# Seven-product stages: the first two sums of weight blocks put together by an accumulating transfer

## The chip, the cores and the metric

The kernel runs on one core of one Trainium2 chip. The metric is the device time of one execution in microseconds (us), the median of several runs. Five engines work side by side, each on its own list of instructions in a fixed order: TensorE (PE; its weight loads are PEld), VectorE (DVE), ScalarE (ACT), GpSimd (POOL) and SyncE (SP). SP and ACT issue transfers; POOL can issue them too.

## The reference

Two layers of an encoder trunk on 512 tokens of width 1024, float32 throughout. Each layer is a half-step feed-forward block, a mixer of three kinds of attention with gates, and a second half-step feed-forward block:

```python
def swiglu(x, w_gu, w_down):
    gate, up = jnp.split(x @ w_gu, 2, axis=-1)
    return (jax.nn.silu(gate) * up) @ w_down

y = swiglu(rmsnorm(h, ffn1_pre_g[l]), ffn1_w_gu[l], ffn1_w_down[l])
h = h + 0.5 * rmsnorm(y, ffn1_post_g[l])
```

`w_gu` is 1024 x 5632 (2816 gate and 2816 up columns), `w_down` 2816 x 1024. Four such blocks are computed, two per layer. The change lies in `x @ w_gu` of these four.

## The kernel before, in words

Activations lie transposed, features on the 128 partitions and tokens along the row. TensorE's float32 products are made from splits: a value is written as a rounded part `hi` (ScalarE copies it into float32r) and the rest `lo` (VectorE subtracts), and a product takes three matmuls: hi·hi, hi·lo, lo·hi. So each block of weights costs a copy on ScalarE and a subtraction on VectorE before TensorE can use it.

Weights come from device memory as tiles of eight 128 x 128 blocks (512 KB) in the order in which they are used: `wts[i]` is the i-th tile. `fetch` loads one into a buffer of the tag `wr`, of which there are three. The tag `wp` has four buffers of 512 KB; the plain products keep split weights in them.

A feed-forward block has 22 pairs of gate and up columns. The first six (`PLAIN`) are plain products. The other 16 are groups of a scheme with seven products in place of eight: rows are halved into two lots of four blocks, tokens into two halves, and gate and up columns are combined. These 16 groups I call a seven-product stage; there are four of them, one in each feed-forward block. The activations' sums and differences are made once, ahead of the stage. For the weights each group g needs:

- two tiles, fetched by SP in `fetches(g)`. The first, `raws[g][0]`, holds the blocks called 22 and 11; the second, `raws[g][1]`, holds 12 in its first half and the base block-column in its second half.
- `sum13` (L543): `r13` = first tile + base, where the base is used for both halves of the first tile. One VectorE instruction of 128 x 1024 elements. `r13` lies in a buffer of `wp`.
- `high13`, `low13` (L555, L559): the split of `r13`.
- `sum2` (L562): the second half of the second tile becomes `r13`'s second half plus the first tile's first half. `sum4` (L572): the first half of the second tile becomes the sum of its two halves.
- `high1`, `low1` (L547, L551), `high12`, `low12` (L566, L569), `high24`, `low24` (L576, L580): the splits of the first tile, of 12 and of the two later sums. `w12` lies in `wp`, the others in the tag `x` (12 buffers).

A group has the products p1 to p7, each of 12 matmuls (L650). In the loop they come in the order p1(g), p7(g), p3(g-1), p6(g), p4(g), p2(g), p5(g). p1 and p4 use the first tile's split, p7 and p5 that of `r13`, p2 that of 12, p6 and p3 that of the two later sums. Partial results stay in PSUM: `seed` (L689), `copy7` (L693) and `copy2` (L696) copy them out between products on ScalarE, `add21` (L700) and `add22` (L704) add them on VectorE, `silu0`, `silu1` (L708, L711) and `gated` (L716) finish a pair of columns. Because p3(g-1) writes the PSUM bank that `add22(g-1)` reads, it waits for it.

The order in the code is not the order on the engines. A planner works through the whole program when it is built and puts each engine's instructions in order by when it reckons their inputs and buffers to be ready, the earlier in the program first. Then each engine works its list through in that order; an instruction that waits holds up all behind it. So the trace shows instructions of group g+2 on VectorE and ScalarE while TensorE is at group g, and `fetches(g+2)`, which stands near the end of iteration g, is on SP ahead of that, as the buffers come free.

The first group's work stands in `first_group`, which runs once all weights of the plain products are split; after it, `sum2(0)`, `low13(0)` and so on stand ahead of the loop.

Of the kernel before, what the change touches and what calls it, by code (L numbers as in the profile page):

```python
# [10 lines left out]
F32 = mybir.dt.float32  # L11
F32R = mybir.dt.float32r
AF = mybir.ActivationFunctionType
ALU = mybir.AluOpType
AX = mybir.AxisListType

P = 128
# [94 lines left out]
def encoder_kernel(ctx: ExitStack, tc: tile.TileContext, order, xT, wts, cols, rows, rpb, consts, tables, out):  # L112
    nc = tc.nc
# [3 lines left out]
    sb = ctx.enter_context(tc.tile_pool(name="sb", bufs=1))  # L117
# [4 lines left out]
    BUFS = {"h": 8, "x": 12, "t": 6, "wr": 3, "wp": 4}  # L122
# [10 lines left out]
    def nm(s):  # L133
        serial[0] += 1
        return f"{s}{serial[0]}"
# [13 lines left out]
    V, A, G, PE = nc.vector, nc.scalar, nc.gpsimd, nc.tensor  # L149
# [23 lines left out]
    HB = WB // 2  # L173
    stream = {"raw": [], "ready": [], "made": 0, "held": {}, "limit": 0, "stop": NTILES * 2, "later": [], "pace": 1}
# [8 lines left out]
    def fetch(parts, eng=nc.scalar):  # L183
        raw = sb.tile([P, WB, P], F32, tag="wr", name=nm("wr"), bufs=BUFS["wr"])
        src = wts[len(stream["raw"])].rearrange("p (a b) -> p a b", b=P)
        for c in range(0, WB, WB // parts):
            cs = slice(c, c + WB // parts)
            eng.dma_start(raw[:, cs, :], src[:, cs, :])
        stream["raw"].append(raw)

    def ensure(n):
        while stream["made"] < min(n, stream["stop"]):
            i = stream["made"]
            if i // 2 == len(stream["raw"]):
                fetch(1)
            raw = stream["raw"][i // 2][:, i % 2 * HB : i % 2 * HB + HB, :]
            if i in stream["held"]:
                hi, lo = stream["held"][i]()
            else:
                hi, lo = wpart("w")  # L200
            A.activation(hi, raw, AF.Copy)  # L201
            V.tensor_tensor(out=lo, in0=raw, in1=f(hi), op=ALU.subtract)  # L202
            stream["ready"].append((hi, lo))
            stream["made"] += 1
# [250 lines left out]
    def ffn(l, which, refresh, X):  # L455
        gu, dn = f"ffn{which}_w_gu", f"ffn{which}_w_down"
        HK, HT = KD // 2, T // 2
# [43 lines left out]
        raw = {"11": n1[:, 0], "12": n1[:, 1], "21": n2[:, 0], "22": n2[:, 1], "t3": n3[:, 0], "t1": n3[:, 1]}  # L501
# [25 lines left out]
        raws, W = {}, {}  # L527

        def fetches(g):
            if g < count:  # L530
                W[g] = {}
                for _ in range(2):
                    fetch(1, nc.sync)
                raws[g] = [t.rearrange("p (a b) c -> p a b c", a=2) for t in stream["raw"][-2:]]

        def wpair(name):
            t = pair(name)
            return t.rearrange("p a (b c) -> p a b c", c=P)

        def sum13(g):  # L540
            W[g]["r13"] = sb.tile([P, 2, HB, P], F32, tag="wp", name=nm("r13"), bufs=BUFS["wp"])
            base = raws[g][1][:, 1].unsqueeze(1).to_broadcast([P, 2, HK, P])
            V.tensor_tensor(out=W[g]["r13"], in0=base, in1=raws[g][0], op=ALU.add)  # L543

        def high1(g):
            W[g]["h1"] = wpair("h1")
            A.activation(W[g]["h1"], raws[g][0], AF.Copy)  # L547

        def low1(g):
            W[g]["l1"] = wpair("l1")  # L550
            V.tensor_tensor(out=W[g]["l1"], in0=raws[g][0], in1=f(W[g]["h1"]), op=ALU.subtract)  # L551

        def high13(g):
            W[g]["h13"] = wpair("h13")
            A.activation(W[g]["h13"], W[g]["r13"], AF.Copy)  # L555

        def low13(g):
            W[g]["l13"] = wpair("l13")
            V.tensor_tensor(out=W[g]["l13"], in0=W[g]["r13"], in1=f(W[g]["h13"]), op=ALU.subtract)  # L559

        def sum2(g):
            V.tensor_tensor(out=raws[g][1][:, 1], in0=W[g]["r13"][:, 1], in1=raws[g][0][:, 0], op=ALU.add)  # L562

        def high12(g):
            W[g]["h12"], W[g]["l12"] = wpart("w12")
            A.activation(W[g]["h12"], raws[g][1][:, 0], AF.Copy)  # L566
# [11 lines left out]
        def low24(g):  # L578
            W[g]["l24"] = wpair("l24")
            V.tensor_tensor(out=W[g]["l24"], in0=raws[g][1], in1=f(W[g]["h24"]), op=ALU.subtract)  # L580
# [9 lines left out]
        def first_group():  # L590
            if stream["made"] < stream["stop"]:
                later.insert(0, first_group)
                return
            assert 2 * len(stream["raw"]) == stream["stop"]
            fetches(0)
            high1(0)
            sum13(0)
            high13(0)

        for b in range(0, HK, 2):  # L600
# [63 lines left out]
        def p1(g):  # L664
            d = groups[g]
            d["a"], d["c"] = bank("mm")[:, :HT], bank("mm")[:, :HT]
            d["b"] = seeds[g % 2][:, :HT]
            product(d["a"], wsel(g, "11"), "11", True, False)

        def p7(g):  # L670
            product(groups[g]["c"], wsel(g, "s3"), "t3", True, False)

        def p6(g):
            product(groups[g]["a"], wsel(g, "s2"), "t2", False, False)

        def p4(g):
            product(groups[g]["c"], wsel(g, "22"), "t4", False, True)
# [4 lines left out]
        def p5(g):  # L682
            product(groups[g]["a"], wsel(g, "s1"), "t1", False, False)

        def p3(g):
            product(groups[g]["a"], wsel(g, "s4"), "22", False, True)

        def seed(g):
            A.activation(groups[g]["b"], groups[g]["a"], AF.Copy)  # L689

        def copy7(g):
            groups[g]["v"] = big("t", name="v")
            A.activation(groups[g]["v"][:, HT:], groups[g]["c"], AF.Copy)  # L693

        def copy2(g):
            A.activation(groups[g]["v"][:, :HT], groups[g]["a"], AF.Copy)  # L696

        def add21(g):
            v = groups[g]["v"][:, :HT]
            V.tensor_tensor(out=v, in0=groups[g]["c"], in1=v, op=ALU.add)  # L700

        def add22(g):
            v = groups[g]["v"][:, HT:]
            V.tensor_tensor(out=v, in0=groups[g]["a"], in1=v, op=ALU.add)  # L704
# [5 lines left out]
        def silu1(g):  # L710
            A.activation(groups[g]["t"][:, HT:], groups[g]["a"], AF.Silu)  # L711

        def gated(g):
            if (PLAIN + g) % 4 == 0:
                new_act()
            V.tensor_tensor(out=act[PLAIN + g], in0=groups[g]["t"], in1=groups[g]["v"], op=ALU.mult)  # L716
# [4 lines left out]
        def room(tag, i, k):  # L721
            t = z(tag)
            parts[k][i], parts[k + 1][i] = t[:, 0, :], t[:, 1, :]

        def cut(k):
            if k % 4 == 0 and k:
                four = z(f"a{k // 4 - 1}", shape=(P, 4, T))
                for i in range(min(4, KF - k)):
                    parts[k + i][1] = four[:, i, :]
            p, q = parts[k]  # L730
            A.activation(p, act[k], AF.Copy)
            V.tensor_tensor(out=q, in0=act[k], in1=f(p), op=ALU.subtract)

        for g in range(count):
            more, last = g + 1 < count, g + 1 == count
            p1(g)
            if g:
                add22(g - 1)
            low24(g)
            if more:  # L740
                high1(g + 1)
            seed(g)
            if more:
                sum13(g + 1)
            p7(g)
            if more:
                high13(g + 1)
                low1(g + 1)
            copy7(g)
            if last:  # L750
                room("l11", 0, 0)
                room("ht3", 1, 0)
                room("lt3", 0, 2)
                cut(0)
                cut(1)
            if g:
                p3(g - 1)
            if more:
                sum2(g + 1)
            if g:  # L760
                silu1(g - 1)
            if more:
                high12(g + 1)
            if g:
                gated(g - 1)
            p6(g)
            if more:
                low13(g + 1)
            else:
                room("ht2", 1, 2)  # L770
                room("lt2", 0, 4)
                cut(2)
                cut(3)
                ensure(stream["made"] + 2)
            copy2(g)
            p4(g)
            add21(g)
            if last:
                p5(g)
                add22(g)  # L780
                room("ht4", 0, 6)
                room("lt4", 0, 8)
                cut(4)
                cut(5)
            p2(g)
            silu0(g)
            if more:
                low12(g + 1)
                sum4(g + 1)
                fetches(g + 2)  # L790
                p5(g)
                high24(g + 1)
# [400 lines left out]
```

## Time and profile before

| what | value |
|---|---|
| median of 3 runs | 2523.39 us (2517.01 to 2523.69) |
| the profiled execution's own time | 2517.49 us |
| its span | 2515.7 us |
| instructions | 38188 |
| busy: PE / DVE / ACT / POOL | 98% / 68% / 50% / 8% |
| moved by transfers | 278.21 MB, mean 111 GB/s |

A group of instructions in the profile is told by line, engine, operation and tiles (written<-read), with its count, busy time, the mean of one, and the time that the engine stood idle just before, with what ended it. A row of the timeline gives start, duration, engine, line, and in brackets the idle time before it. A row of the windows gives the stretch, its length, the busy time and count of PE, PEld, DVE, ACT and POOL, the granted clock, the share of time in which the 16 DMA engines were busy, and GB/s. A row of the waits gives who waited for whom, the time in total, how often, and the longest.

### The profile page before, as it was taken

What the parts mean: (1) busy time and instruction counts of PE and PEld (TensorE: products, weight loads), DVE (VectorE), ACT (ScalarE), POOL (GpSimd) and SP (SyncE); (2) the same over time, 40 slices, a digit from 0 to 9 for tenths busy, and PEclk for the clock granted to TensorE, in tenths of its full rate; (3) what the DMA queues carried; (4) which work ended last, traced back from release to release, by engine and by line L of the source; (5) the groups of instructions that cost most, each with busy time, mean ns of one, the idle gap of its engine ahead of it and who ended that gap; (6) DMA issues with size and microseconds to landing.
All of it is one profiled execution on the core that took longest, in us unless ns stands there. A gap on an engine that the chain in (4) does not pass through costs nothing.

```text
span 2515.7 us, 38188 instructions
## 1 busy us (share of the span) xinstructions
PE 2471.4 (98%) x14586; PEld 2181.1 (87%) x14586; DVE 1702.3 (68%) x3062; ACT 1260.5 (50%) x2447; POOL 197.6 (8%) x177
## 2 busy tenths in 40 slices
PE   9999999999999999999999999999999999999998
PEld 8999888888778889998889998888787788899987
DVE  8877248857767478773388772588676764887723
ACT  6555245645555455553355553546455554555532
POOL 0000020000111120000100000200011112100002
PEclk9999999999999999999999999999999999999999
DMA  4333337434443323333233333374344423233232
GB/s 153 109 106 97 100 101 208 115 109 127 117 126 98 108 65 116 101 101 93 92 93 109 110 93 93 125 197 116 107 126 133 119 90 110 65 116 103 91 103 84
DMA packets 97398, 278.21 MB, mean 111 GB/s; under 512 B 13504, under 2 KB 17984, under 8 KB 97216
## 3 DMA queue, kind: packets, MB, share of 16 engines
q10 hardware_dynamic: 41184, 149.52, 19.5%
q1 hardware_dynamic: 56032, 126.27, 17.7%
q8 instruction: 114, 1.87, 0.3%
q14 instruction: 68, 0.56, 0.1%
HBM read 231.16 MB, written 6.29 MB: 94 GB/s over the span
## 4 chain that ended last, share of the span: by engine, by line
PE 85%; DVE 7%; DMA 4%; issue 1%; SPq 1%; ACT 1%; POOL 1%; POOLq 0%; DVEq 0%; ACTq 0%
PE mm L650 19%; PE mm L248 14%; PE mm L247 14%; PE mm L246 14%; PE at L246 4%; PE at L247 4%; PE at L248 4%; PE at L650 3%; DMA wr<-in_wts_dram 1%; DVE X L317 1%; DMA sh<-raw 1%; PE at L884 1%; DVE y L413 1%; PE at L856 1%; PE o L888 1%
## 5 line engine op out<-in xcount | busy, mean ns | idle before, releaser
L202 DVE TENSOR_TENSOR w<-wr,w 128x512 fp32r<-128x512 f32 x568 | 406.6, 721 | 408.7 <-ACT w L201 406.6
L201 ACT ACTIVATE w<-wr 128x512 fp32r<-128x512 f32 x568 | 354.3, 629 | 554.1 <-PE at L248 269.3
L248 PE MATMUL mm<-X,w 128*128 128x512 f32 (+1 forms) x1096 | 418.5, 383 | 7.2 <-DVE w L202 7.2
L247 PE MATMUL mm<-X,w 128*128 128x512 f32 (+1 forms) x1096 | 419.0, 383 | 4.2 <-DVE X L317 4.2
L246 PE MATMUL mm<-X,w 128*128 128x512 f32 (+1 forms) x1096 | 419.3, 384 | 2.9 <-ACT w L201 1.8
L650 PE MATMUL mm<-lt,h 128*128 128x256 f32 x1024 | 289.8, 283 | 0.0
L650 PE MATMUL mm<-ht,h 128*128 128x256 f32 x1024 | 289.8, 283 | 0.0
L650 PE MATMUL mm<-ht,l 128*128 128x256 f32 x1024 | 289.8, 283 | 0.0
L248 PEld LDWEIGHTS mm<-X,w 128*128 128x128 f32 x1096 | 209.8, 192 | 41.5 <-DVE w L202 8.4
L247 PEld LDWEIGHTS mm<-X,w 128*128 128x128 f32 x1096 | 210.1, 192 | 39.2 <-DVE X L317 6.4
L246 PEld LDWEIGHTS mm<-X,w 128*128 128x128 f32 x1096 | 210.0, 192 | 36.2 <-ACT w L201 2.0
L650 PEld LDWEIGHTS mm<-lt,h 128*128 128x128 f32 x1024 | 196.0, 191 | 0.0
L650 PEld LDWEIGHTS mm<-ht,l 128*128 128x128 f32 x1024 | 196.0, 191 | 0.0
L650 PEld LDWEIGHTS mm<-ht,h 128*128 128x128 f32 x1024 | 196.0, 191 | 0.0
L543 DVE TENSOR_TENSOR r<-wr,wr 128x1024 f32<-128x1024 f32 x64 | 78.5, 1226 | 117.9 <-DMA wr<-in_wts_dram 115.1
L311 POOL TENSOR_TENSOR ss<-ss,sq 128x512 f32<-128x512 f32 (+1 forms) x38 | 47.3, 1245 | 1357.6 <-ACT sq L310 1356.5
L247 PE MATMUL mm<-a,w 128*128 128x512 f32 (+1 forms) x432 | 152.7, 354 | 0.0
L650 PE MATMUL mm<-h,h 128*128 128x256 f32 x512 | 145.7, 285 | 3.4 <-DVE v L704 3.3
L650 PE MATMUL mm<-h,l 128*128 128x256 f32 x512 | 144.9, 283 | 0.0
L650 PE MATMUL mm<-l,h 128*128 128x256 f32 x512 | 144.9, 283 | 0.0
L271 ACT ACTIVATE hi<-at 128x256 fp32r<-128x256 f32 (+2 forms) x168 | 76.5, 473 | 73.1 <-PE at L884 29.4
L247 PE MATMUL mm<-lo,w 128*128 128x512 f32 (+1 forms) x288 | 110.6, 384 | 0.0
(270 smaller groups left out, 5814.7 us busy)
## 6 DMA issues: line engine op xcount, KB each, us to landing
wr<-in_wts_dram ACTq DMA_DIRECT2D x285, 512.0 KB, 3.5
wr<-in_wts_dram SPq DMA_DIRECT2D x130, 512.0 KB, 3.5
st<-hi SPq DMA_DIRECT2D x84, 128.0 KB, 2.4
st<-lo SPq DMA_DIRECT2D x84, 128.0 KB, 3.3
sh<-raw SPq DMA_DIRECT2D x104, 64.0 KB, 3.4
sw<-lo SPq DMA_DIRECT2D x36, 128.0 KB, 3.8
sw<-hi SPq DMA_DIRECT2D x36, 128.0 KB, 2.7
braw<-in_rpb_dram SPq DMA_DIRECT2D x16, 256.0 KB
```

The lines of the kernel that those rows point to most:

```text
L201: A.activation(hi, raw, AF.Copy)
L202: V.tensor_tensor(out=lo, in0=raw, in1=f(hi), op=ALU.subtract)
L246: PE.matmul(acc, w[0], x[0], start=start, stop=False)
L247: PE.matmul(acc, w[0], x[1], start=False, stop=False)
L248: PE.matmul(acc, w[1], x[0], start=False, stop=stop)
L271: A.activation(hi, src, AF.Copy)
L311: eng.tensor_tensor(out=self.acc[:, cs], in0=self.acc[:, cs], in1=sq[:, cs], op=ALU.add)
L317: V.scalar_tensor_tensor(out=lo[:, hs], in0=h[b][:, hs], scalar=gcol(b), in1=f(hi)[:, hs], op0=ALU.mult, op1=ALU.subtract)
L413: V.tensor_tensor(out=y[b][:, hs], in0=y[b][:, hs], in1=reps[i], op=ALU.mult)
L543: V.tensor_tensor(out=W[g]["r13"], in0=base, in1=raws[g][0], op=ALU.add)
L650: PE.matmul(acc, ws[i], xs[j], start=start and k == n == 0, stop=stop and k == HK - 1 and n == 2, skip_group_check=True,)
L856: PE.matmul(sp, qs, sk[0][:, j0 * P : j1 * P], start=True, stop=False)
```

## The change

`sum13` and its calls go away. Instead, `fetches(g)`, after the two fetches, takes the buffer for `r13`, has SP copy the base half of the second tile from device memory into both halves of it, and has GpSimd issue a transfer that adds the whole first tile, again from device memory, onto what lies there.

```diff
@@ fetches(g)
                 for _ in range(2):
                     fetch(1, nc.sync)
                 raws[g] = [t.rearrange("p (a b) c -> p a b c", a=2) for t in stream["raw"][-2:]]
+                at = len(stream["raw"]) - 2
+                two, base = (wts[i].rearrange("p (a b c) -> p a b c", a=2, b=HB) for i in (at, at + 1))
+                W[g]["r13"] = sb.tile([P, 2, HB, P], F32, tag="wp", name=nm("r13"), bufs=BUFS["wp"])
+                for i in range(2):
+                    nc.sync.dma_start(W[g]["r13"][:, i], base[:, 1])
+                G.dma_start(W[g]["r13"], two, accum_op=ALU.add)
@@
-        def sum13(g):
-            W[g]["r13"] = sb.tile([P, 2, HB, P], F32, tag="wp", name=nm("r13"), bufs=BUFS["wp"])
-            base = raws[g][1][:, 1].unsqueeze(1).to_broadcast([P, 2, HK, P])
-            V.tensor_tensor(out=W[g]["r13"], in0=base, in1=raws[g][0], op=ALU.add)
@@ first_group
             fetches(0)
             high1(0)
-            sum13(0)
             high13(0)
@@ the loop over groups
             seed(g)
-            if more:
-                sum13(g + 1)
             p7(g)
             if more:
                 high13(g + 1)
```

A group reads 1 MB more from device memory: 2 x 256 KB for the base and 512 KB for the first tile. `r13`'s buffer is now taken in `fetches(g)`, up to a loop iteration earlier in the program than before.

## The prediction, made before the result was known

> **What bounds the kernel now.** I read the page first: busy time, the chain that ended last, the costliest groups. Then the four seven-product stages by windows, then who waits for whom, then one group instruction by instruction.
>
> ```profile
> span 2515.7 us, 38188 instructions
> PE 2471.4 (98%) x14586; PEld 2181.1 (87%) x14586; DVE 1702.3 (68%) x3062; ACT 1260.5 (50%) x2447; POOL 197.6 (8%) x177
> PE 85%; DVE 7%; DMA 4%; issue 1%; SPq 1%; ACT 1%; POOL 1%; POOLq 0%; DVEq 0%; ACTq 0%
> L543 DVE TENSOR_TENSOR r<-wr,wr 128x1024 f32<-128x1024 f32 x64 | 78.5, 1226 | 117.9 <-DMA wr<-in_wts_dram 115.1
> ```
>
> TensorE sets the time. The sum that the change takes away (L543) costs VectorE 64 x 1.226 = 78.5 us, and VectorE stands idle longer than that, 117.9 us, just before it. So the question is what these 78.5 us are worth to TensorE inside the stages where they lie:
>
> ```profile
> 76.79:239.34 162.55, 161.66 (x1345) 161.25 (x1343) 127.27 (x168) 87.89 (x156) 0.00 (x0) 1.00 0.34 104
> 971.11:1133.20 162.09, 161.63 (x1344) 161.22 (x1343) 127.20 (x168) 87.50 (x156) 0.00 (x0) 1.00 0.34 105
> 1329.94:1493.00 163.06, 161.72 (x1345) 161.31 (x1344) 127.31 (x168) 88.30 (x156) 0.00 (x0) 1.00 0.34 104
> 2219.22:2381.60 162.38, 161.65 (x1344) 161.24 (x1343) 127.14 (x168) 88.00 (x156) 0.00 (x0) 1.00 0.34 105
> sum 650.08, PE 646.65 PEld 645.01 DVE 508.92 ACT 351.69 POOL 0.00; mean PE 161.66 PEld 161.25 DVE 127.23 ACT 87.92 POOL 0.00
> PE mm L650 <- DVE v L704: 3.3, 7, 1.1
> ```
>
> Columns: window, length, busy PE, weight load, VectorE, ScalarE, GpSimd, clock, DMA share, GB/s. In the four stages together TensorE is idle 650.08 - 646.65 = 3.4 us, and 3.3 of it is one wait: for the addition `add22` (L704). Whatever VectorE is spared, these stages can give back about 3.4 us, 0.14% of the time.
>
> So the change can hardly gain; can it lose? That is read from one group in the steady part. I call the group whose `r13` is made at 153.00 n; TensorE meanwhile works on n-2, 10.08 us a group.
>
> ```profile
> 145.74 0.28 PE L650 MATMUL at<-h,w 128*128 128x256 f32 x1
> 146.07 0.33 SPq L188 DMA_DIRECT2D wr<-in_wts_dram  x1
> 149.44 0.33 SPq L188 DMA_DIRECT2D wr<-in_wts_dram  x1
> 152.99 0.63 ACT L566 ACTIVATE w<-wr 128x512 fp32r<-128x512 f32 x1
> 153.00 1.23 DVE L543 TENSOR_TENSOR r<-wr,wr 128x1024 f32<-128x1024 f32 x1 [2.12 <-DMA wr<-in_wts_dram]
> 154.14 0.69 DVE L716 TENSOR_TENSOR a<-t,v 128x512 f32<-128x512 f32 x1
> 154.74 1.22 DVE L580 TENSOR_TENSOR l<-wr,h 128x1024 fp32r<-128x1024 f32 x1
> 155.54 1.04 ACT L555 ACTIVATE h<-r 128x1024 fp32r<-128x1024 f32 x1
> 155.88 0.42 DVE L700 TENSOR_TENSOR v<-mm,v 128x256 f32<-128x256 f32 x1
> 156.21 0.68 DVE L562 TENSOR_TENSOR wr<-r,wr 128x512 f32<-128x512 f32 x1
> 156.81 0.68 DVE L569 TENSOR_TENSOR w<-wr,w 128x512 fp32r<-128x512 f32 x1
> 157.53 0.69 DVE L572 TENSOR_TENSOR wr<-wr 128x512 f32<-128x512 f32 x1
> 158.14 1.22 DVE L551 TENSOR_TENSOR l<-wr,h 128x1024 fp32r<-128x1024 f32 x1
> 159.08 0.37 ACT L689 ACTIVATE at<-mm 128x256 f32<-128x256 f32 x1 [2.22 <-PE mm L650]
> 159.27 0.42 DVE L704 TENSOR_TENSOR v<-mm,v 128x256 f32<-128x256 f32 x1
> 160.26 0.28 PE L650 MATMUL mm<-h,h 128*128 128x256 f32 x1
> ```
>
> The two fetches of group n are issued at 146.07 and 149.44; the second lands just ahead of 153.00, 3.5 us on. From there VectorE runs a closed train to `add22` of n-2, which ends at 159.27 + 0.42 = 159.69; product p3 of n-2, which waits for it, begins at 160.26. **The margin is 0.57 us.** `sum2` (L562) reads `r13` and stands in this train. So it must begin by 156.21 + 0.57 = 156.8 if the order behind it stays as it is.
>
> **The change part by part.** *Removed:* the sum L543, 1.23 us a group of VectorE. Worth to TensorE: between 0 and 3.4 us in all; I take 3, since the only wait it can shorten is at L704, early in each stage.
>
> *Added on SP:* two copies of 256 KB a group, each 0.33 us of issue (the rows at 146.07). SP waits for buffers most of each group, so the issue itself costs nothing; if it did not wait, it would be 0.66 us of 10.08. They come in the program behind the two fetches and need a buffer of `wp`, of which there are four. At 152.99 three of these hold `w12` of n-2, n-1 and n, so one is left for `r13`; the buffer for `r13` of n comes free when p2 of n-3 has read its `w12`. That is the last row with at<-h,w, 145.74 + 0.12 = 145.9. The copies can thus be issued between 145.9 (ahead of the fetch at 146.07) and 146.4 to 146.7 (behind it). The fetch and the later one behind them on SP then wait for the same buffer as well; as it is free by 145.9 this moves them by at most the 0.66 us of issue.
>
> ```profile
> 149.44:150.40 0.96, 0.96 (x10) 0.96 (x9) 0.96 (x2) 0.02 (x1) 0.00 (x0) 1.00 0.06 4
> 150.40:152.60 2.20, 2.20 (x21) 2.20 (x20) 0.48 (x1) 1.26 (x2) 0.00 (x0) 1.00 0.72 236
> wr<-in_wts_dram SPq DMA_DIRECT2D x130, 512.0 KB, 3.5
> kept<-h SPq DMA_DIRECT2D x16, 256.0 KB, 3.9
> h<-kept SPq DMA_DIRECT2D x16, 256.0 KB, 2.5
> ```
>
> A fetch takes 0.96 us to its first packets, 2.2 us of packets, and 3.5 - 3.16 = 0.3 us to its landing. The two copies are 512 KB more, so 2.2 us of packets: ahead of the fetch they land at about 145.9 + 0.96 + 2.2 + 0.3 and a little for the fetch between, 149.9 in all; behind it at 146.07 + 0.96 + 4.4 + 0.3, with the second fetch's packets from 150.4 on, 152.0.
>
> *Added on GpSimd:* one accumulating transfer of 512 KB, which waits for both copies. GpSimd does nothing in these stages (the 0.00 above), so nothing is queued behind this wait. No row shows such a transfer. From below it is a plain fetch, 3.5 us. From above, two of them one after the other, 7.0. It must read what lies in the buffer as well as the weights, so I take one fetch plus its packets once more: 3.5 + 2.2 = 5.7. `r13` then is there at 149.9 + 3.5 = 153.4 at the earliest, 152.0 + 7.0 = 159.0 at the latest, and by my values at 152.0 + 5.7 = 157.7; I take the order behind the fetch because that is the program's.
>
> [...]
>
> *Moved: who waits for `r13`.* ScalarE's `high13` (L555) goes from 155.54 to 157.7; behind it are `silu0` and the seed at 159.08: 157.7 + 1.04 + 0.37 = 159.1, just covered. VectorE's `sum2` begins 157.7 instead of 156.8 at the latest: 0.9 us late, and behind it L569, L572, L551 and `add22`. The delay reaches p3 of n-2, and four products later p2 of n-1, on whose end the copies of n+2 wait. One such round spans two groups, so 0.9 us is 0.45 us a group. With some of it taken back by `low12` slipping ahead I take 0.4. The first four groups of a stage run otherwise, with VectorE short of time; for the other 12 or 13, 52 in all, that is **+21 us**; by the ends, 0 (153.4) and (159.0 - 156.8)/2 x 52 = +57.
>
> *At the entry of a stage* there is no lead:
>
> ```profile
> 68.37 1.23 DVE L543 TENSOR_TENSOR r<-wr,wr 128x1024 f32<-128x1024 f32 x1 [0.67 <-PE mm L248]
> 67.12 0.33 SPq L188 DMA_DIRECT2D wr<-in_wts_dram  x1
> 78.22 0.28 PE L650 MATMUL mm<-ht,h 128*128 128x256 f32 x1
> ```
>
> The first `r13` waits for a `wp` buffer that the plain products give back (L248), at 68.3. Now the copies start there, behind the packets of the fetch of 67.12 (68.1 to 70.3): packets to 72.5, landed by 72.9; `r13` at 78.6, with `high13` and `low13` (1.04 + 1.22) 80.9. Product p7 wants them at 78.22: 2.6 us late, four times, **+10 us**. From below: copies landed by 72.0, 3.5 us more, 77.8: nothing. From above 72.9 + 7.0 + 2.3 = 82.2: 4 x 4.0 = 16.
>
> *Traffic:* 1 MB more a group on top of 1 MB at a DMA share of 0.34, with the second read some 0.85. The fetches get later by some of it; the second one at 152.99 feeds `high12`, and this has no idle time to lose beyond about 1.9 us. I put nothing for it.
>
> **Sum:** -3 + 21 + 10 = +28 us. The profiled execution took 2517.5 us (span 2515.7), 5.9 below the median of the runs, 2523.4. On the profile's own time it gives 2545.5; for the median I say **2551 us**.
>
> **The rivals.**
>
> *In time.* The accumulating transfer is as quick as a fetch, or the copies go ahead of the fetch: `r13` by 153.4 to 156.8. Then TensorE loses nothing in the steady part, 0 to 5 us at the entries, and gets up to 3.4 back: 2520 to 2525. For it: 10 us of lead in which SP mostly waits. Against it: each link of the chain has to be at its lower end.
>
> *The relief pays.* This ends on the other side: VectorE, shorter by 1.23 us a group, is ahead at `add22` in the first groups, and the planner, with room on VectorE, also draws the splits (`cut`) for the down projection forward out of the following stage. It gains the 3.4 us, and has to find over 4 us more elsewhere: 2514. It decides only if `r13` is there by 155. Against it: the wait rows name no other place where VectorE's sum delays TensorE.
>
> *The planner puts `sum2` early.* If it reckons `r13` ready when the second fetch lands, `sum2` goes to 153.0 ahead of L716, L580 and L700. Then the whole train hangs on `r13`: 157.7 plus the train without L543, 159.69 - 154.14 = 5.5, gives 163.2 against 160.26, 2.9 us in two groups, 52 x 1.5 = +76, with the entry 2606. For it: it is ready when data is. Against it: L716 and L580 stand earlier in the program and are ready at the same time.
>
> *The accumulation is slow.* If it takes 10 us, `r13` is there at 162: (162 - 156.8)/2 x 52 = 135, entries 4 x 7 = 28: about 2685. No row bears on it.
>
> **How the numbers follow.** Late by a little (forecast) 0.42; in time 0.30; relief 0.05; early `sum2` 0.09; slow accumulation 0.14. The range 2514 to 2606 leaves out the slow case and a little below. About 0.3%, 7.6 us, is what can be told from no change. Faster 0.05, from the relief alone; within 0.3% 0.30; slower 0.65. The forecast's own range is 2530 to 2580.
>
> **What would show it.** Right: TensorE's waits on L650 grow from 3.4 to some 25 us, for L704 and for L551/L559; VectorE's idle time stands before L562 with a DMA as the releaser, and no longer before L543; GpSimd's transfer takes 5 to 6 us to land; the first p7 of each stage waits about 2.6 us; the DMA share of the stages doubles. Wrong: a landing under 4 us with L562 never waiting (in time), or L562 ahead of L716 in VectorE's order. If the stages keep their 650 us and the time still moves, the cause lies where I have not looked.

## The result, and the profile after

The changed kernel takes 2620.38 us (median; 2610.13 to 2624.34), the kernel before, run beside it, 2523.54 us (2517.01 to 2527.35). The ratio is 1.038, with a 95% interval of 1.034 to 1.042: the change costs 97 us. The prediction said 2551 us with a range of 2514 to 2606: the sign was right, the size was not.

The page of the changed kernel. Lines below `high1` have moved: `high13` is L556, `low13` L560, `sum2` L563, `low1` L552, `high24` L577; the copies are L539, GpSimd's transfer is L540; the product (L650) and `add22` (L704) are where they were.

```profile
span 2618.4 us, 38722 instructions
PE 2506.5 (96%) x14586; PEld 2204.1 (84%) x14586; DVE 1633.7 (62%) x2998; ACT 1264.2 (48%) x2447; POOL 253.2 (10%) x241
PE 71%; DMA 15%; DVE 8%; issue 3%; ACT 1%; SPq 1%; POOL 1%; POOLq 0%; DVEq 0%; ACTq 0%
...
L563 DVE TENSOR_TENSOR wr<-r,wr 128x512 f32<-128x512 f32 x64 | 44.3, 692 | 183.2 <-DMA r<-in_wts_dram 163.6
L540 POOL DMA_DIRECT2D r<-in_wts_dram x64 | 55.4, 865 | 830.1 <-DMA r<-in_wts_dram 379.3
...
wr<-in_wts_dram SPq DMA_DIRECT2D x130, 512.0 KB, 4.2
r<-in_wts_dram SPq DMA_DIRECT2D x128, 256.0 KB, 4.1
r<-in_wts_dram POOLq DMA_DIRECT2D x64, 512.0 KB, 6.7
```

VectorE is busy 68.6 us less, as intended, and TensorE's time is worse. Of the chain that ended last, 15% is now DMA, where it was 4%. VectorE stands idle 183.2 us ahead of `sum2` (L563), nearly all of it for the transfer into `r13`. The columns of the last rows are count, size and median us from issue to landing: GpSimd's accumulating transfer takes 6.7 us, and the fetch 4.2 where it took 3.5.

The four seven-product stages by windows, and TensorE's waits on L650:

```profile
76.77:264.95 188.18, 171.06 (x1346) 167.49 (x1345) 117.36 (x158) 92.40 (x159) 12.95 (x15) 0.96 0.67 178
1006.31:1192.52 186.21, 171.04 (x1346) 167.88 (x1345) 117.29 (x158) 92.14 (x159) 12.90 (x15) 0.96 0.68 180
1387.61:1575.27 187.66, 170.71 (x1346) 167.53 (x1345) 117.39 (x158) 92.36 (x159) 12.95 (x15) 0.96 0.67 178
2301.59:2484.38 182.79, 168.38 (x1346) 165.77 (x1345) 117.23 (x158) 92.86 (x159) 12.93 (x15) 0.97 0.69 183
sum 744.84, PE 681.18 PEld 668.67 DVE 469.27 ACT 369.76 POOL 51.73; mean PE 170.30 PEld 167.17 DVE 117.32 ACT 92.44 POOL 12.93
```

```profile
PE mm L650 <- DVE v L704: 34.7, 32, 4.3
PE mm L650 <- ACT h L556: 16.5, 4, 4.8
PE mm L650 <- ACT v L696: 8.3, 3, 3.3
PE mm L650 <- ACT h L577: 3.6, 3, 1.9
```

The stages grew from 650.08 to 744.84 us, 94.8 of the 102.7 us by which the span grew. This splits in two. TensorE's idle time is 744.84 - 681.18 = 63.7 us, 60.2 more than before; the waits above name 63.1 of it. And its busy time, for the same matmuls, is 681.18 instead of 646.65, 34.5 us more. The larger part of this is the clock: the granted clock is 0.96 and 0.97 where it was 1.00, TensorE runs at half clock for 51 us, 6 of them while it stands, and half of the other 45 is some 22 us. The remaining 12 us are not the clock's: e3 below has them too (busy 659.03 us in its stages, 12.4 more than before) with only 3.4 us of half clock. What they are I leave open. The prediction has no term for either part. The other 8 us lie outside the stages: the stretch from the first stage to the second, which holds layer 0's mixer, takes 741.6 instead of 731.8 us (from the last L650 of one to the first of the next); the other two stretches moved by 1.3 us or less.

By groups, from the starts of the L650 matmuls (what each gap exceeds 0.12 us, the pace at full clock): before, the four stages lose 5.5 us; after, 99.1. Of these, 60 us fall into groups 0 to 3 of the stages and 39 into groups 4 to 15. The prediction had 10 and 21. Within the 60, the first round of the loop has 34.6 us, the second none, the third and fourth have 25.7 together.

The entry of the first stage and one group of its steady part, from the timeline:

```profile
68.35 0.80 SPq L539 DMA_DIRECT2D r<-in_wts_dram  x2
73.47 1.00 POOL L540 DMA_DIRECT2D r<-in_wts_dram  x1 [72.52 <-DMA r<-in_wts_dram]
80.58 0.69 DVE L563 TENSOR_TENSOR wr<-r,wr 128x512 f32<-128x512 f32 x1 [8.10 <-DMA r<-in_wts_dram]
80.58 1.06 ACT L556 ACTIVATE h<-r 128x1024 fp32r<-128x1024 f32 x1 [8.15 <-DMA r<-in_wts_dram]
81.69 0.58 PE L650 MATMUL mm<-ht,h 128*128 128x256 f32 x1 [4.53 <-ACT h L556]
82.07 0.42 PE L650 MATMUL mm<-lt,h 128*128 128x256 f32 x1
...
186.89 1.85 SPq L539 DMA_DIRECT2D r<-in_wts_dram  x2
188.78 0.69 DVE L563 TENSOR_TENSOR wr<-r,wr 128x512 f32<-128x512 f32 x1 [3.40 <-DMA r<-in_wts_dram]
192.18 0.42 DVE L704 TENSOR_TENSOR v<-mm,v 128x256 f32<-128x256 f32 x1
192.38 0.86 POOL L540 DMA_DIRECT2D r<-in_wts_dram  x1 [10.13 <-DVE l L552]
192.65 0.39 PE L650 MATMUL mm<-h,h 128*128 128x256 f32 x1 [1.47 <-DVE v L704]
198.69 0.81 SPq L539 DMA_DIRECT2D r<-in_wts_dram  x2
198.98 0.69 DVE L563 TENSOR_TENSOR wr<-r,wr 128x512 f32<-128x512 f32 x1 [1.81 <-DMA r<-in_wts_dram]
```

In the steady part it is the ring that was forecast: copies issued when p2 gives the buffer back (186.89), GpSimd's transfer (192.38), `sum2` when it lands (198.98), 12.1 us in all; and from the `sum2` of the group before (188.78) over `add22` (192.18) and p3 (192.65) to the end of a p2 and the copies for the second group after it (198.69), 9.9 us. One round is 22.0 us for two groups that TensorE alone would do in 20.16. At the entry, though, VectorE and ScalarE both stand for 8 us in front of an instruction that reads `r13`, and TensorE for 4.5.

### The profile page after: what moved, and what is told of

The parts are those of the page before. It is cut to its first block, busy times and chain, and to the rows that moved or that the text cites. A ratio compares the mean times of both kernels' runs of the same rounds, so it can differ in the third digit from the quotient of the medians.

```text
span 2618.4 us, 38722 instructions
## 1 busy us (share of the span) xinstructions
PE 2506.5 (96%) x14586; PEld 2204.1 (84%) x14586; DVE 1633.7 (62%) x2998; ACT 1264.2 (48%) x2447; POOL 253.2 (10%) x241
## 4 chain that ended last, share of the span: by engine, by line
PE 71%; DMA 15%; DVE 8%; issue 3%; ACT 1%; SPq 1%; POOL 1%; POOLq 0%; DVEq 0%; ACTq 0%
PE mm L248 13%; PE mm L247 13%; PE mm L246 13%; DMA r<-in_wts_dram 10%; PE mm L650 9%; PE at L246 4%; PE at L247 4%; PE at L248 4%; DMA wr<-in_wts_dram 3%; PE at L650 2%; DVE l L552 2%; DVE X L317 1%; PE at L882 1%; DMA sh<-raw 1%; DVE y L413 1%
## 5 line engine op out<-in xcount | busy, mean ns | idle before, releaser
L650 PE MATMUL mm<-ht,h 128*128 128x256 f32 x1024 | 296.6, 290 | 28.4 <-ACT h L556 16.5
L650 PE MATMUL mm<-ht,l 128*128 128x256 f32 x1024 | 294.2, 287 | 0.0
L650 PE MATMUL mm<-lt,h 128*128 128x256 f32 x1024 | 294.0, 287 | 0.0
L650 PEld LDWEIGHTS mm<-ht,h 128*128 128x128 f32 x1024 | 201.4, 197 | 31.8 <-ACT h L556 17.3
L650 PEld LDWEIGHTS mm<-lt,h 128*128 128x128 f32 x1024 | 201.4, 197 | 0.0
L650 PEld LDWEIGHTS mm<-ht,l 128*128 128x128 f32 x1024 | 201.0, 196 | 0.1
L650 PE MATMUL mm<-h,h 128*128 128x256 f32 x512 | 153.4, 300 | 35.0 <-DVE v L704 34.7
L563 DVE TENSOR_TENSOR wr<-r,wr 128x512 f32<-128x512 f32 x64 | 44.3, 692 | 183.2 <-DMA r<-in_wts_dram 163.6
L650 PE MATMUL mm<-h,l 128*128 128x256 f32 x512 | 149.8, 293 | 0.3 <-DVE l L552 0.3
L650 PE MATMUL mm<-l,h 128*128 128x256 f32 x512 | 148.6, 290 | 0.0
L650 PEld LDWEIGHTS mm<-h,h 128*128 128x128 f32 x512 | 101.6, 198 | 43.2 <-DVE v L704 42.4
L540 POOL DMA_DIRECT2D r<-in_wts_dram x64 | 55.4, 865 | 830.1 <-DMA r<-in_wts_dram 379.3
L581 DVE TENSOR_TENSOR l<-wr,h 128x1024 fp32r<-128x1024 f32 x64 | 78.4, 1225 | 83.0 <-ACT h L577 83.0
```

Source lines behind the costliest of these rows:

```text
L540: G.dma_start(W[g]["r13"], two, accum_op=ALU.add)
L650: PE.matmul(acc, ws[i], xs[j], start=start and k == n == 0, stop=stop and k == HK - 1 and n == 2, skip_group_check=True,)
```

## The experiments

All ratios are to the kernel before, run on the same chip beside them.

### e1: what adding costs

The chain, the sizes and the waits stay, but GpSimd's transfer overwrites `r13` with the first tile instead of adding it; the sum is left out.

```diff
-                G.dma_start(W[g]["r13"], two, accum_op=ALU.add)
+                G.dma_start(W[g]["r13"], two)
```

> The transfer that GpSimd issues copies the first tile instead of adding it; the two copies ahead of it, its waits and its size stay. The sums are left out, so r13 holds the first tile alone. Theory (r13 comes late through a chain of buffer, copies, GpSimd's own waits and a transfer of 6.7 us, and stops of TensorE are then lengthened by the halved clock behind them): without the second read the transfer lands in some 4.5 us instead of 6.7, r13 is there about 2.2 us sooner, and most of the 94 us lost in the four stages come back: 2540 to 2565 us. Rival A (the added traffic slows the fetches): the traffic from memory is the same, so 2600 to 2625 us. Rival B (the planner's other order costs the time, whatever lands when): 2600 to 2625 us.

Measured: 2545.94 us (2540.57 to 2546.41), ratio 1.009 (1.007 to 1.012). From its page:

```profile
r<-in_wts_dram SPq DMA_DIRECT2D x128, 256.0 KB, 3.5
r<-in_wts_dram POOLq DMA_DIRECT2D x64, 512.0 KB, 4.5
```

A plain transfer lands in 4.5 us, an adding one in 6.7: the addition costs 2.2 us a group, as much as the 2.2 us of packets that the prediction charged once more. The chain from buffer to `sum2` falls to 9.6 to 10.3 us in groups 8 to 15 of the first stage, groups 6 to 15 then lose next to nothing, and three quarters of the loss are gone.

### e2: a transfer that is in time

The copies are left out too, and GpSimd brings the first tile alone into `r13`'s buffer, so that it waits for no copy. What is measured is VectorE without its sum, with `r13` early.

```diff
-                for i in range(2):
-                    nc.sync.dma_start(W[g]["r13"][:, i], base[:, 1])
-                G.dma_start(W[g]["r13"], two, accum_op=ALU.add)
+                G.dma_start(W[g]["r13"], two)
```

> As the run before, and the two copies by SP are left out as well: r13 is one plain transfer of 512 KB issued by GpSimd as soon as the buffer is free. It leaves out both sums. Theory: the chain loses the 4.1 us of the copies and about 1 us of GpSimd's waits for them, so r13 is there before sum2 wants it: 2515 to 2530 us. Rival A: half of the added traffic is left, so about half of the loss: 2565 to 2580 us. Rival B: the planner's order is still another one: over 2580 us.

Measured: 2516.96 us (2512.28 to 2521.27), ratio 0.998 (0.996 to 0.999); the stages lose 0.6 us each. So 78 us less on VectorE are worth 0.2% at the best, about the 3.4 us that the waits of the kernel before had to give. It also shows a transfer issued by GpSimd, with half of the change's added traffic, to be harmless as such.

### e3 and e6: the later groups alone, and the first four alone

e3 makes the change for groups 4 to 15, e6 for groups 0 to 3; in the others VectorE adds as before.

```diff
@@ fetches(g), behind the two fetches
+                if g < FROM:
+                    return
@@ sum13(g), which is kept
+            if g >= FROM:
+                return
```

`FROM` is 4; in e6 both comparisons are turned round.

> The change for groups 4 to 15 of each stage alone; groups 0 to 3 are summed by VectorE as before. Theory: of the 99 us that TensorE loses in the stages 60 lie in the first four groups, where r13 has no lead and the stops bring the clock down; they go away: 2550 to 2570 us. Rival A (traffic, in proportion to the groups): a quarter goes away, about 2596 us.

> The change made for groups 0 to 3 of each stage alone; from group 4 on VectorE adds as before. Theory (the loss of the first groups is their own: there is no lead, r13 is late at once, and the stops are long enough to halve the clock): in the changed kernel the first four groups lose 60 us over the four stages, so 2520 + 60 = 2580 us, between 2565 and 2590, with windows of half clock at 3 or 4 stage entries and no waits of TensorE from group 6 or so on. As the prediction priced the entry (10 us): 2530 us. Rival A (the loss goes with the traffic, 16 of 64 groups): 2520 + 25 = 2545 us, with no halved clock.

Measured: e3 2562.93 us (2559.78 to 2565.61), ratio 1.016 (1.014 to 1.019), 42.6 us over its kernel before; e6 2572.14 us (2568.5 to 2575.0), ratio 1.022 (1.020 to 1.024), 54.0 us over its own. Together 96.6 us, and the whole change costs 96.8. The two parts stand beside each other, and the smaller number of groups carries the larger loss: 13.5 us at each entry. In e6 the loss is over by group 6, and its added traffic is a quarter of the change's; a loss that goes with the traffic would have been 24 us.

### e4: one buffer more

`wp` gets a fifth buffer (`t` gives one up, and pads shrink to make room), so that the copies can go out about a group earlier.

```diff
-PAD = {"f": 184, "m": 184}
+PAD = {"f": 8, "m": 8}
...
-    BUFS = {"h": 8, "x": 12, "t": 6, "wr": 3, "wp": 4}
+    BUFS = {"h": 8, "x": 12, "t": 5, "wr": 3, "wp": 5}
```

> The change as it is with five buffers of the tag wp instead of four (paid for with one buffer of the tag t and the padding). Theory: the copies no longer wait for p2 to give a buffer back and go out about 3 us sooner, so that r13 has 12 us of lead instead of 9: no loss in the steady part, half of it at the entry: 2530 to 2565 us. Rival A: traffic is the same, 2600 to 2625 us. Rival C (GpSimd's transfer cannot be hidden, as it takes longer the more is in flight): 2590 to 2620 us.

Measured: 2579.32 us (2574.38 to 2586.4), ratio 1.022 (1.019 to 1.025). All expectations missed; it lies between those of the chain and of the traffic, and its page says why:

```profile
L563 DVE TENSOR_TENSOR wr<-r,wr 128x512 f32<-128x512 f32 x64 | 44.3, 692 | 231.6 <-DMA wr<-in_wts_dram 150.0
...
wr<-in_wts_dram SPq DMA_DIRECT2D x130, 512.0 KB, 5.2
r<-in_wts_dram SPq DMA_DIRECT2D x128, 256.0 KB, 4.8
r<-in_wts_dram POOLq DMA_DIRECT2D x64, 512.0 KB, 6.9
```

With the copies out earlier, the transfers crowd more (in a steady group the second fetch leaves at 183.62 and the copies at 185.09 and 185.47, beside GpSimd's transfer of 181.42 that lands at 188.60), and the fetches land in 5.2 us. Of the 231.6 us that VectorE now stands in front of `sum2`, 150.0 end with the second fetch and no longer with `r13`. So with the chain loosened the fetches are the next limit, 41 us below the first. How much of what is left comes from the buffer that `t` gave up, no run shows.

### e5: the same bytes off every chain

The kernel before; in each group SP also stores two finished tiles of 512 KB to scratch.

```diff
         def high1(g):
             W[g]["h1"] = wpair("h1")
             A.activation(W[g]["h1"], raws[g][0], AF.Copy)
+            nc.sync.dma_start(dr.tile([P, 2, HB, P], F32, tag="spill", name=nm("spill"), bufs=8), f(W[g]["h1"]))
```

(and the same for `h13`)

> The kernel before, with nothing taken from VectorE and no step made to wait: in every group SyncE only stores two finished tiles of 512 KB (h1 and h13) to a scratch area, which nothing reads. This is 1 MB a group beside the 1 MB of fetches, as in the change, but off every chain. Theory (the chain of buffer, copies, GpSimd's transfer makes r13 late, and late r13 stops TensorE long enough to halve its clock): the fetches land some 0.5 to 0.7 us later, as in the changed kernel (4.2 us), which the margin of 0.57 us at add22 nearly covers: 2518 to 2535 us, stages almost free of idle time. Rival A (the traffic is what costs: the fetches come late): most of the loss is here too, 2570 to 2610 us, with fetches landing in 5 us or more.

Measured: 2511.74 us (2505.14 to 2515.35), ratio 0.997 (0.996 to 0.998). Rows of its page, and its first stage as a window, then that of e1:

```profile
wr<-in_wts_dram SPq DMA_DIRECT2D x130, 512.0 KB, 3.6
spill<-h SPq DMA_DIRECT2D x128, 512.0 KB, 3.5
```

```profile
77.18:238.62 161.44, 161.44 (x1346) 161.44 (x1345) 128.09 (x168) 90.85 (x156) 0.00 (x0) 1.00 0.59 203
```

```profile
77.20:244.59 167.39, 163.52 (x1346) 162.02 (x1345) 117.28 (x158) 93.08 (x159) 7.96 (x15) 1.00 0.64 199
```

203 GB/s beside the matmuls, more than in the changed kernel (178 to 183), and the fetch still lands in 3.6 us, where it took 3.5 in the kernel before: that many bytes a second did not slow the fetches by themselves. These are stores, where the change reads. But e1 reads all that the change reads, at 199 GB/s in its first stage, and its fetches land in 3.7 us. With the adding they land in 4.2 us, the DMA engines busy 0.67 to 0.69 of the time for fewer bytes a second; with the transfers crowded (e4), in 5.2. That this run is a little faster than the kernel before was not expected; e11 follows it up.

### e7: one copy instead of two

```diff
-                for i in range(2):
-                    nc.sync.dma_start(W[g]["r13"][:, i], base[:, 1])
+                nc.sync.dma_start(W[g]["r13"], base[:, 1].unsqueeze(1).to_broadcast([P, 2, HB, P]))
```

> The changed kernel with its two copies of the base made by one transfer of 512 KB that reads the base twice. Bytes are the same, but SyncE issues once instead of twice (0.33 us less) and GpSimd has one semaphore fewer to wait for ahead of its transfer (some 0.5 us less). Theory (the loss is set by the chain from the buffer to r13): the chain is 0.5 to 0.9 us shorter, worth 0.25 to 0.45 us a group in the 48 later groups (12 to 22 us), and less at the entries: 2590 to 2608 us. Rival A (bytes decide): as the changed kernel, 2612 to 2626 us.

Measured: 2605.56 us (2604.7 to 2612.17), ratio 1.035 (1.033 to 1.038). In the band of the chain, but by luck: the interval overlaps that of the change, and the chain from the copy to `sum2`, which was to be 0.5 to 0.9 us shorter, is 11.7 us in the mean of groups 8 to 15, as in the change. The stages lose 90.2 us instead of 99.1, 8.9 less and not 12 to 22, and the other half of the gain lies in layer 0's mixer (733.1 instead of 741.6 us). The joint copy lands in 4.7 us where the two landed in 4.1, which eats the wait and the issue that were saved. So this run does not test the chain; e1 and e2 do.

### e8: the sum on GpSimd's own arithmetic

No transfer; the kernel before with one word changed.

```diff
-            V.tensor_tensor(out=W[g]["r13"], in0=base, in1=raws[g][0], op=ALU.add)
+            G.tensor_tensor(out=W[g]["r13"], in0=base, in1=raws[g][0], op=ALU.add)
```

> The kernel before, with the same sum made by an instruction of GpSimd instead of VectorE: no copies, no added traffic, no transfer, VectorE freed of the same 78 us. GpSimd's additions of 128x512 took 1.3 to 1.7 us before, so this one of 128x1024 should take 2.6 to 3.4 us and end 155.6 to 156.4 on the scale of the prediction's group, ahead of the 156.8 that sum2 can bear. Theory (the traffic and the chain of the change cost, not the freeing of VectorE): 2512 to 2525 us, same as before or up to 0.25% faster, stages under 2 us of idle time each. Rival (any r13 that VectorE doesn't make is late in the first groups): 2530 to 2550 us. If additions on GpSimd slow those on VectorE that run beside them, VectorE's rows get longer and the stages lose more than that.

Measured: 2557.14 us (2555.66 to 2557.48), ratio 1.016 (1.014 to 1.018). The main expectation missed; the last sentence of it holds. First a row of the kernel before (groups by form, 130 to 240 us), then of e8 (the same view), then three of e8's timeline:

```profile
L716 DVE TENSOR_TENSOR a<-t,v 128x512 f32<-128x512 f32 x10 | 6.8, 684 | 0.0
```

```profile
L716 DVE TENSOR_TENSOR a<-t,v 128x512 f32<-128x512 f32 x11 | 29.7, 2696 | 0.0
```

```profile
170.24 1.23 DVE L580 TENSOR_TENSOR l<-wr,h 128x1024 fp32r<-128x1024 f32 x1 [1.63 <-ACT h L576]
170.90 2.83 POOL L543 TENSOR_TENSOR r<-wr,wr 128x1024 f32<-128x1024 f32 x1 [7.70 <-DMA wr<-in_wts_dram]
171.38 2.90 DVE L716 TENSOR_TENSOR a<-t,v 128x512 f32<-128x512 f32 x1
```

The one instruction of VectorE that begins while GpSimd adds (`gated`, a multiplication) takes 2.7 us instead of 0.68 and ends just after GpSimd's has ended (173.73); all its neighbours keep their times. So VectorE gets 1.23 us a group and pays 2.0 in the same train, and the period goes from 10.08 to 10.53 us. That is not the whole loss: of the 44 us that its stages lose, 24 lie in groups 0 to 3, where TensorE's longest waits are for the seed (L689, 10.5 us in four waits), so an `r13` that is late at the entry, the rival's cause, has a part in it too. What holds `gated` up, no run shows.

### e9, e10, e12: is it the stop that halves the clock?

28 idle matmuls (3.4 us) fill TensorE's first wait of each stage: in e9 (e6's kernel) and e10 (the changed kernel) ahead of the first p7, in e12 (e6's kernel) ahead of the first p1. They write the bank that p7 starts anew.

```diff
         def p1(g):                                  # e9, e10: in p7(g)
+            if g == 0:
+                for _ in range(28):
+                    PE.matmul(d["c"], W[g]["h1"][:, 1][:, 0, :], hi["11"][:, 0, :], start=True, stop=True, skip_group_check=True)
             product(d["a"], wsel(g, "11"), "11", True, False)
```

> The change for groups 0 to 3 alone, and between the first group's p1 and p7 TensorE makes 28 idle matmuls (3.4 us) into the bank of p7, which p7 then starts anew: nothing of the result changes. Without them (2572 us) TensorE stood still for 3.5 to 4.7 us there, and its clock was halved for 3.4 to 6.8 us (20.4 us over the four entries, 10 us lost). Theory (the stop is what halves the clock): the wait is filled, the clock stays whole at the four entries, and 8 to 10 us come back: 2560 to 2566 us. Rival (the halving has another cause, or it costs nothing because r13's lateness decides anyway): 2570 to 2576 us. If the clock stays whole and the time does not move, the wait for the next r13 has taken what the clock gave.

> The changed kernel with the same 28 idle matmuls ahead of the first p7 of each stage. Theory: the clock stays whole at the entries (the halved stretches after the first waits were 6.8, 6.8, 6.8 and 3.4 us long, 23.8 in all, 11.9 us lost); the later stops in groups 1 to 7 stay. 2620 - 8 to 12 = 2608 to 2612 us if it all comes back, 2620 if the chain of buffers takes it again.

> The change for groups 0 to 3 alone, with 28 idle matmuls (3.4 us at full clock) once more, now ahead of the first p1 of each stage, since in the run before this one (e9) TensorE went into its wait after only four of them: p1's third matmul wants the low part of the first tile, and low1 stands on VectorE behind sum2, which waits for r13. So the waits of 3.5 to 4.7 us at the four entries shrink to 0.1 to 1.4 us. Theory (the stop halves the clock; 20 us of halved clock at the entries, 10 us lost): no half-clock stretch within 8 us of the four entries, and against 2572 us some 5 to 10 us less, 2562 to 2567 us; the rest is taken by the next late r13. Rival (the halving has another cause): stretches of half clock at the entries as before, 2570 to 2576 us.

Measured: e9 2582.97 us (2580.24 to 2584.26), ratio 1.024 (1.022 to 1.026); e10 2625.76 us (2620.07 to 2629.27), ratio 1.040 (1.038 to 1.043). Both miss, because the fill stood in the wrong place: in e9's first entry only four of the 28 ran ahead of the wait, which is p1's own (its third matmul wants `low1(0)`, and that stands on VectorE behind `sum2(0)`). The other 24 ran after it, partly at half clock (0.50 from 82.8 to 86.2), and were paid in full. These two runs say nothing of the clock's cause, but they show that the first wait is not p7's alone.

e12: 2567.94 us (2566.52 to 2573.78), ratio 1.020 (1.018 to 1.022), 47.7 us over its kernel before where e6 lost 54.0; the intervals overlap. Its first entry:

```profile
76.61 3.52 PE L681 MATMUL mm<-h,h 128*128 128x256 f32 x28
82.20 0.38 PE L661 MATMUL mm<-h,l 128*128 128x256 f32 x1 [1.84 <-DVE l L562]
82.42 0.28 PE L661 MATMUL mm<-h,h 128*128 128x256 f32 x1
90.25 0.58 PE L661 MATMUL mm<-ht,h 128*128 128x256 f32 x1 [4.86 <-ACT at L703]
82.18 0.33 SPq L189 DMA_DIRECT2D wr<-in_wts_dram  x1
88.35 0.63 ACT L577 ACTIVATE w<-wr 128x512 fp32r<-128x512 f32 x1 [4.51 <-DMA wr<-in_wts_dram]
```

```profile
82.20:85.10 2.90, 2.86 (x21) 2.66 (x22) 2.90 (x4) 1.06 (x1) 0.02 (x1) 1.00 0.80 109
88.00:94.80 6.80, 4.55 (x21) 4.55 (x22) 5.44 (x6) 4.33 (x8) 0.86 (x1) 0.50 0.61 122
```

The wait that was filled has shrunk from 4.62 to 1.84 us (at the other entries to 1.28, 0.15 and 1.22), and the matmuls behind it run at full clock (0.28 us each, window 1.00), where e6 had half. But the next wait follows at once: the seed (L703) on ScalarE stands behind `high12` of group 1 (L577), whose tile could be fetched only when `sum2(0)` and `low1(0)` had given a buffer back (82.18) and landed at 88.35. In e6 the planner had put the seed first. TensorE stops for 4.86 us, and now the half clock (0.50) comes with that stop, 88.0 to 94.8. It is so at all four entries: the second wait lasts 3.1 to 4.9 us, and the halved stretch begins 2.6 to 4.8 us after the start of that stop. So the expectation of no half clock at the entries missed, and the halving moved with the stop, which is what tells the stop from another cause. The time hardly followed (the spans of the two profiled executions are 2567.0 and 2566.7 us): the late `r13` also holds the buffers of the fetches, and with the other order on ScalarE the seed waits for them.

### e11: the order on VectorE alone

In e5 the planner had put `add22` ahead of `low1`. This is the kernel before with only that.

```diff
                 high13(g + 1)
-                low1(g + 1)
             copy7(g)
...
             add21(g)
+            if more:
+                low1(g + 1)
```

> The kernel before, with low1 of the next group moved behind add21 in the program, so that add22 may go ahead of it on VectorE, as it did in the run with the stores (2511.7 us against 2518.2). Nothing else is changed. If that order is what made that run faster: stages without idle time (5.5 us less) and 2511 to 2515 us. If the gain there came from elsewhere (the mixers, where its clock was halved once and not five times): 2515 to 2522 us.

Measured: 2511.76 us (2507.6 to 2514.47), ratio 0.996 (0.994 to 0.997), 0.4% faster than the kernel before. The sum over its windows of the four stages, and a piece of VectorE's train:

```profile
sum 645.68, PE 645.68 PEld 645.68 DVE 510.61 ACT 361.30 POOL 0.00; mean PE 161.42 PEld 161.42 DVE 127.65 ACT 90.33 POOL 0.00
```

```profile
155.93 0.69 DVE L572 TENSOR_TENSOR wr<-wr 128x512 f32<-128x512 f32 x1
156.54 0.42 DVE L704 TENSOR_TENSOR v<-mm,v 128x256 f32<-128x256 f32 x1
156.87 1.22 DVE L559 TENSOR_TENSOR l<-r,h 128x1024 fp32r<-128x1024 f32 x1
158.00 1.22 DVE L551 TENSOR_TENSOR l<-wr,h 128x1024 fp32r<-128x1024 f32 x1
```

`add22` ends at 156.96 instead of 159.69, with VectorE doing its whole sum, and TensorE is never idle in the stages: 645.68 us of 645.68. What the change wanted from VectorE, there was to be had by order, without moving any work. The stages give 4.4 of the 9.9 us by which the span shrank (650.08 to 645.68); 3.6 lie in the stretch with layer 0's mixer (728.2 instead of 731.8), whose cause I did not follow.

## Why the prediction was wrong in size and right in sign

*What bounds the kernel, and the 3.4 us to be won: right.* e2 gets 0.2% with `r13` in time, and e11 shows the same idle time gone.

*The rival "in time": right under its condition.* e2 is that case and comes out 3.4 us under its kernel before, at the lower edge of what the rival said (2520 from 2523.4). The condition does not hold with copies and an adding transfer in the chain. *Early `sum2`* and *slow accumulation* did not happen: `sum2` stands behind L716 and L580 as forecast, and the transfer took 6.7 us. *The relief pays* needs `r13` by 155; in the change `sum2` waits for the transfer in 53 of 64 groups.

*The chain from the free buffer to `r13`: right in sum, by errors that cancel.* Forecast 145.9 to 157.7, 11.8 us; measured between 11.1 and 12.6 in groups 8 to 15 of the first stage. The copies landed sooner (4.1 us from issue, by the 20 of 128 whose landing the trace has, not 5.3 to 5.6). The second is issued some 0.4 us after the first, and GpSimd, which waits for up to three semaphores in a row (160 for its 64 transfers), starts its transfer 0.56 us after the second copy's landing (in 13 of the 14 groups that show it), terms I did not have. And the transfer takes 6.7 us, not 5.7; of its two parts, the packets once more were right in size (2.2 by e1; that they are a second read, no row shows), the base was short: a plain one of GpSimd's takes 4.5, not the 3.5 of SP's fetch.

*"With some of it taken back by `low12` slipping ahead I take 0.4" (+21 us): the mechanism right, the size half.* Groups 4 to 15 lose 39 us in the change and 42.6 alone (e3), 0.8 to 0.9 us a group. The round is the forecast one, but nothing was taken back (`low12`, L570, stands behind `sum2` as before), and its second half takes 9.9 us (188.78 to 198.69) where the rows of before give 145.9 + 20.16 - 156.8 = 9.3; about 0.3 of it is `add21` (L700), which the planner now has behind `sum2`. The bound that I wrote down, 57 us, holds it.

*"Product p7 wants them at 78.22: 2.6 us late, four times, +10 us": this is the step that failed.* It measured 54 us (e6, groups 0 to 3 alone). Even the part that it priced came out larger: TensorE's first waits, 2.6 us each in the forecast, are 16.5 us in four (L556), and the first round of the loop loses 34.6 us. Three things were left out of it; no run gives each its own price. First, I priced TensorE's wait alone and not the engines behind it. In the entry's rows VectorE and ScalarE stand 8.1 us in front of `sum2(0)` and `high13(0)`; what is queued behind them is `low1(0)` (so even p1 stops, as e9 showed), the last plain columns, and the next group's splits. Second, I took the lead to be missing for the first `r13` only. Groups 1 to 3 have none either: VectorE starts them with its 8 us of arrears, the buffers come free late, and so the copies and the fetches go out late (SP's next fetch after that of 67.1 leaves at 82.44, in the kernel before at 71.49). The third and fourth rounds lose 25.7 us, where the kernel before loses 5.5. The prediction said that these groups "run otherwise, with VectorE short of time", and then gave them no number. Third, half clock follows the stops, 51 us of it in the stages.

*The clock: not foreseen.* It is some 22 of the 34.5 us by which TensorE's busy time grew in the stages. In the stages of the kernel before it never happened; the longest stop there was 1.1 us.

*Traffic at nothing: no run contradicts it for the change as it stands, but there is a limit behind it.* e5 carries a higher rate at no cost. The fetches did get later, 3.5 to 4.2 us, and the second fetch has little to spare: in e4 the fetches decide. The forecast DMA share of 0.85 was 0.67 to 0.69.

*Outside the stages* the change adds 8 us that the prediction has nowhere, all in the stretch with layer 0's mixer. No run of the experiments has them there (726.8 to 734.8 us), not even e10, which is the changed kernel with 28 matmuls more a stage, so they are not shown to come from the change at all. The stretches of half clock there are 23.8 us long together, 17.0 before, which is 3.4 us of the 9.8; the rest I leave open. Shifts of this size come and go among the runs: the stretch with layer 1's mixer takes 724.7 to 737.3 us in them.

## What to carry to other kernels

When work moves from an engine to a transfer, price the whole chain (buffer free, copies, waits of the issuing engine, transfer), and then everything that is queued behind each reader of the result, on every engine: at the entries without lead, of the 54 us that e6 lost, TensorE's first waits were 16.9. The 78.5 us that VectorE was busy with the sum said nothing of what relieving it was worth; the 3.3 us of waits that named it did (e2 gained 3.4), and a swap of two instructions in its order gave all that the relief could have given (e11: no idle time of TensorE in the stages).

## What the runs showed of the hardware

**Half clock with TensorE's stops.** In the fourteen traces, of the stops of TensorE longer than 3 us, 39 of 40 are followed, within 6.5 us of their start, by a stretch of granted clock 0.50, which mostly lasts 3.4 or 6.8 us; of those of 2 to 3 us, 29 of 43; of 1.5 to 2 us, 25 of 101. So are some shorter ones: of the 136 such stretches, 36 begin within 6.5 us of no stop longer than 1.5 us, and all of one longer than 1 us. Such a row of the changed kernel, around its first stop:

```profile
80.00:90.00 10.00, 8.31 (x43) 7.92 (x44) 7.53 (x10) 4.80 (x7) 1.01 (x2) 0.66 0.58 160
```

This stop lasted 4.53 us, to 81.69, and the half clock from 81.1 to 87.9, which is some 3.1 us more for the 6.2 us of it in which TensorE works, an estimate from that length; within the changed kernel's stages the clock was halved for 51 us. What else decides whether a stop is followed by it, these counts do not show.

**A transfer that GpSimd issues** takes 4.5 us for 512 KB where SP's takes 3.7 in the same run (e1), and 6.7 when it adds into SBUF; each adding issue holds GpSimd for 0.86 us, a plain one for 0.53.

**VectorE beside GpSimd's arithmetic**: `gated`, which begins while GpSimd adds, takes 2.7 us, where it takes 0.68 in the kernel before (e8).
